# First k-tile's shift and scale by matmuls on TensorE in a hybrid retention layer, with a new order of loads, norms and copies in the front

## The chip, the cores and the metric

The kernel runs on one core of one Trainium2 chip. The metric is device time in microseconds (us) of one launch, the median of several runs. The engines are TensorE (PE; its weight loads are shown as PEld), VectorE (DVE), ScalarE (ACT), GpSimd (POOL) and SyncE (SP), which issues most of the DMAs. TensorE's clock has two levels, 1.2 and 2.4 GHz; the profile's column PEclk shows the granted clock as a share of the full one.

## What is computed

One layer over 512 latent tokens of width 1024, with 256 context tokens and two conditioning vectors of length 1024. The part that the change touches is the start:

```python
mod   = jax.nn.silu(c)     @ w_ada + b_ada      # 6 * 1024 columns
mod_c = jax.nn.silu(c_ctx) @ w_ada + b_ada
sh1, sc1, g1, sh2, sc2, g2 = jnp.split(mod[:, None, :], N_MOD, axis=-1)
sh1c, sc1c, ... = jnp.split(mod_c, N_MOD, axis=-1)

uc = _modulate(ctx, sh1c, sc1c)                 # _layer_norm(.) * (1 + scale) + shift
...
u = _modulate(x, sh1, sc1)
mix = _token_mixer(u @ w_in, ...)               # retention, pooling, gates, projections
x = _post_norm(ALPHA * x + g1 * mix, ...)
...                                             # modulation, gated MLP with a convolution, post norm
```

## The kernel before

Features lie on the partitions in all large products: `x` (512 x 1024) is loaded in four blocks of 128 rows, normalised, and transposed on TensorE into `xnT`, eight k-tiles of 128 features by 512 tokens. The modulated `u` is split into a high and a low part (`uh`, `ul`), as each weight tile is (`hi`, `lo`), and each product is made in three passes: `wh*uh`, `wl*uh`, `wh*ul`. The conditioning columns lie in `mod` (128 x 48): column j holds features 128j to 128j+127 of silu(c) @ w_ada + b_ada. `mod` column kt is the shift of k-tile kt, column 8+kt its scale. `modc` holds the same for the context, 16 columns.

The front of the program, from the first load to the end of the k-tile loop, stands inside `ordered(*ORDS)`: on each of the five engines the instructions keep the order in which the program writes them. So a line that is moved in the source is moved on its engine's queue, and whatever stands behind a waiting instruction waits too. The order in the source of before is this:

- `load_x`, `load` of c, ident and bada, and `first_load(0)` (L242 to L254) put the loads on SP's queue.
- For each row block, `x_stats` (L280) takes statistics on VectorE (L132, L123); GpSimd makes the reciprocal root (L125, L126) and the product L283. `x_norm` (L286) is one instruction: on ScalarE (L290) it waits for L283, on VectorE (L292) for L126. `x_trans(tb, g)` (L294) transposes one half of a block, four 128 x 128 transposes into one PSUM bank (L298), and a copy on ScalarE puts them into `xnT` (L318 to L350).
- `silu_row` (L108) broadcasts silu(c) over the partitions by eight transposes into two banks (L117), and ScalarE copies them into an SBUF row (L118). The dot products of the front read the banks; later ones read the row.
- `warm(n)` (L301) issues n filler matmuls in bf16 on zeros (L304).
- `first_matvec(j)` (L255) makes one column of `mod`: two products with sum of 128 x 512 on VectorE (L258), and L260 adds the parts and the bias.
- The first k-tile is prepared in L329 to L349: `uh` on ScalarE (L339), the weights' casts (L341) and low parts, `u` (L344) and the subtraction for `ul` (L83) on VectorE. `held` are transposes whose copies come later (L350, L367).
- The loop over the eight k-tiles (L359) has TensorE's 18 matmuls of a k-tile in `g0_mm` (L352, L356), 6 feature tiles by 3 passes, and prepares the next k-tile by `first_prep` (L267): the weights' split (cast on ScalarE L88, low part on GpSimd L83), two calls of `first_matvec`, and `modulate` (L225, L228). At k-tile 6 `ctx_mod(0)` (L387) makes the context's columns 0 and 8 on VectorE.

Behind the loop come the other projections, `mm3` (L92 to L95), the retention, and the MLP. `L641` and `L644` are small fp32 matmuls of the retention: the loop at L643 issues four of L644 per head.

## Time and profile before

| | us |
|---|---|
| median of 3 runs | 829.94 |
| lowest, highest | 828.57, 830.37 |
| the profiled execution's own time | 828.57 |
| its span in the profile | 826.8 |
| TensorE busy | 801.3 |
| VectorE busy | 537.5 |
| GpSimd busy | 401.6 |
| ScalarE busy | 365.1 |

The profile shows one execution, the fastest of the three. Its span runs from the first to the last instruction; the run's own time has 1.77 us more around it. A busy TensorE is not one at its peak, since its ends are modelled. In the rows further down, "idle before <-releaser" is the time for which the engine had nothing to do before that instruction, and what ended it.

### The profile page before, as it was taken

The numbers are of one execution on the slowest core, as the hardware profiler recorded it, in microseconds if no ns is written. First come the engines' busy times: TensorE is split into PE (matmuls) and PEld (weight loads), VectorE is DVE, ScalarE is ACT, GpSimd is POOL, SyncE is SP. The second block draws the span as 40 slices with busy tenths as digits, with TensorE's granted clock in tenths as the row PEclk, the third lists the DMA queues.
The fourth block names the chain that finished last, engine by engine and source line by source line (L and its number), as shares of the span: only waits on it lengthen the run. The fifth ranks groups of instructions, "written<-read, shape, count | busy, mean of one in ns | idle before, by whom it ended". The sixth has DMA issues, their size and how long they took to land.

```text
span 826.8 us, 10600 instructions
## 1 busy us (share of the span) xinstructions
PE 801.3 (97%) x3865; PEld 668.9 (81%) x3865; DVE 537.5 (65%) x1040; ACT 365.1 (44%) x579; POOL 401.6 (49%) x295
## 2 busy tenths in 40 slices
PE   6989999999999999999999999999999999999995
PEld 4768877888888888888788998888888888888884
DVE  7947789884267773333667579887778877522147
ACT  4644526221454343323325476665566556233101
POOL 3754360021443242104624779988888888321106
PEclk9999999999999999999999999999999999999998
DMA  9950359973220006460504512322232222343002
GB/s 342 405 199 1 140 205 328 324 259 120 75 77 26 1 2 253 133 201 9 205 21 185 192 38 85 117 83 97 103 103 102 83 97 102 102 153 102 1 1 101
DMA packets 34356, 106.94 MB, mean 129 GB/s; under 512 B 4592, under 2 KB 5376, under 8 KB 34304
## 3 DMA queue, kind: packets, MB, share of 16 engines
q1 hardware_dynamic: 34304, 106.27, 36.7%
q8 instruction: 30, 0.49, 0.2%
q14 instruction: 22, 0.18, 0.1%
HBM read 104.14 MB, written 2.11 MB: 129 GB/s over the span
## 4 chain that ended last, share of the span: by engine, by line
PE 87%; DVE 5%; POOL 2%; ACT 2%; issue 2%; DMA 1%; POOLq 0%; SPq 0%; DVEq 0%; ACTq 0%
PE ps L95 26%; PE ps L94 26%; PE ps L93 26%; PE ps L356 3%; PE ps L674 1%; PE ps L644 1%; PE ps L675 1%; POOL S L83 1%; DVE raw L205 1%; DVE S L258 1%; DVE lo L83 1%; PE ps L636 1%; DMA S<-in_x 1%; PE ps L641 1%; POOL lo L83 1%
## 5 line engine op out<-in xcount | busy, mean ns | idle before, releaser
L95 PE MATMUL ps<-S,lo 128*128 128x512 f32 (+1 forms) x560 | 216.4, 388 | 4.2 <-POOL lo L83 3.2
L93 PE MATMUL ps<-S,hi 128*128 128x512 f32 (+1 forms) x560 | 218.2, 390 | 1.0 <-ACT hi L88 1.0
L94 PE MATMUL ps<-S,hi 128*128 128x512 f32 (+1 forms) x560 | 217.1, 388 | 0.0
L83 POOL TENSOR_TENSOR lo<-raw,hi 128x1024 fp32r<-128x1024 f32 (+3 forms) x61 | 141.2, 2317 | 154.6 <-ACT hi L88 152.0
L998 DVE SCALAR_TENSOR_TENSOR t<-ps,convw,t 128x441 f32<-128x441 f32 (+1 forms) x258 | 163.8, 690 | 45.3 <-POOL t L996 45.1
L88 ACT CAST hi<-raw 128x1024 fp32r<-128x1024 f32 (+1 forms) x96 | 99.3, 1035 | 176.1 <-PE ps L95 61.3
L95 PEld LDWEIGHTS ps<-S,lo 128*128 128x128 f32 x560 | 105.6, 189 | 26.9 <-POOL lo L83 4.0
L93 PEld LDWEIGHTS ps<-S,hi 128*128 128x128 f32 x560 | 105.5, 188 | 22.6 <-ACT hi L88 1.5
L94 PEld LDWEIGHTS ps<-S,hi 128*128 128x128 f32 x560 | 105.6, 189 | 21.2
L996 POOL TENSOR_TENSOR t<-t,t 128x448 f32<-128x448 f32 x88 | 101.9, 1158 | 34.4 <-ACT t L1081 31.0
L95 PE MATMUL ps<-S,S 128*128 128x512 f32 (+1 forms) x308 | 112.2, 364 | 0.0
L94 PE MATMUL ps<-S,S 128*128 128x512 f32 (+1 forms) x308 | 112.2, 364 | 0.0
L93 PE MATMUL ps<-S,S 128*128 128x512 f32 (+1 forms) x308 | 111.4, 365 | 0.0
L83 DVE TENSOR_TENSOR lo<-raw,hi 128x1024 fp32r<-128x1024 f32 x37 | 47.2, 1276 | 68.0 <-ACT hi L88 68.0
L94 PE MATMUL ps<-lo,S 128*128 128x512 f32 x208 | 81.0, 390 | 0.0
L95 PE MATMUL ps<-hi,S 128*128 128x512 f32 x208 | 80.8, 389 | 0.0
L93 PE MATMUL ps<-hi,S 128*128 128x512 f32 x208 | 77.2, 391 | 1.6 <-ACT S L546 1.0
L83 POOL TENSOR_TENSOR S<-raw,S 128x1024 fp32r<-128x1024 f32 x21 | 50.6, 2410 | 38.9 <-ACT S L765 23.5
L1078 ACT ACTIVATE t<-ps,convb,convw 128x512 f32<-128x512 f32 x43 | 33.6, 781 | 75.2 <-PE ps L95 75.2
L93 PEld LDWEIGHTS ps<-S,S 128*128 128x128 f32 x308 | 58.1, 189 | 9.2
L94 PEld LDWEIGHTS ps<-S,S 128*128 128x128 f32 x308 | 58.1, 189 | 9.2
L95 PEld LDWEIGHTS ps<-S,S 128*128 128x128 f32 x308 | 58.1, 189 | 9.1
(219 smaller groups left out, 1065.3 us busy)
## 6 DMA issues: line engine op xcount, KB each, us to landing
raw<-in_w_up SPq DMA_DIRECT2D x44, 512.0 KB, 3.3
raw<-in_wada SPq DMA_DIRECT2D x32, 512.0 KB, 5.3
raw<-in_w_down SPq DMA_DIRECT2D x22, 512.0 KB, 3.3
S<-in_wada SPq DMA_DIRECT2D x16, 512.0 KB, 9.6
raw<-in_w_v SPq DMA_DIRECT2D x16, 256.0 KB, 4.5
raw<-in_w_ga SPq DMA_DIRECT2D x8, 512.0 KB, 4.3
raw<-in_w_gb SPq DMA_DIRECT2D x8, 512.0 KB, 3.3
raw<-in_w_br SPq DMA_DIRECT2D x8, 512.0 KB, 4.0
```

The costliest lines, as they stand in the source:

```text
L83: eng.tensor_tensor(out, x, y, ALU.subtract)
L88: act.copy(hi, raw)
L93: pe.matmul(out, lhsT=sh, rhs=mh, start=first, stop=False)
L94: pe.matmul(out, lhsT=sh, rhs=ml, start=False, stop=False)
L95: pe.matmul(out, lhsT=sl, rhs=mh, start=False, stop=last)
L205: dve.scalar_tensor_tensor(out_junk, raw, 1.0, silu_c, ALU.mult, ALU.mult, accum_out=mod[:, j:j + 1])
L258: dve.scalar_tensor_tensor(junk[:, cs], ada_slot(j)[:, cs], 1.0, silu_h[hf], ALU.mult, ALU.mult, accum_out=dst[:, j:j + 1])
L356: pe.matmul(g0[f], lhsT=w[:, f * P:(f + 1) * P], rhs=m[:, kt, :], start=kt == 0 and i == 0, stop=kt == NKT - 1 and i == 2)
L636: pe.matmul(score[h + i][:, ns], lhsT=kT[half_rows, t, ns], rhs=qT[half_rows, t, ns], start=True, stop=True)
L996: pool.tensor_tensor(o, o, i, ALU.add)
L998: dve.scalar_tensor_tensor(o, i, w, o, ALU.mult, ALU.add)
L1078: act.activation(acc, src, AF.Identity, bias=convb[:, i:i + 1], scale=convw[:, i, 4:5])
```

## The change

- `w_ada`'s tiles 0 and 8 come to the device transposed (`wada_t`), and `c` and `c_ctx` as two columns for each k. `pe_matvec(i)` makes shift (i = 0) and scale (i = 1) of the first k-tile by eight matmuls of 128 x 2 each on TensorE, which add up in a bank `mv`, for c and c_ctx at once. `put_matvec` adds the bias on VectorE. The two calls of `first_matvec` for k-tile 0 go, and with them `ctx_mod(0)` at k-tile 6.
- c, ident and bada are loaded from ScalarE's queue; SP begins with the four blocks of x.
- Block 0's norm goes from VectorE to ScalarE, in halves; the first half of block 2's from ScalarE to VectorE. `x_trans(0, 1)` stands earlier. The last group of fillers, `warm(N_W)`, goes.
- `first_u` makes `uh` and `u` of the first k-tile in pieces of 384 and 128 columns; the second reads the bank of block 3's transposes.
- ScalarE's two copies of silu's banks into the SBUF row stand behind the copies of the held transposes in the loop's first turn.

```diff
--- before.py
+++ after.py
@@ -105,9 +105,8 @@
     dve.memset(neg_half, -0.5)
     keep("gap0", [P, 24])
 
-    def silu_row(cols):
-
-        t = row()
+    def silu_banks(cols):
+
         halves = []
         for hf in range(2):
             ps = bank()
@@ -115,8 +114,7 @@
             for j in range(4):
                 k = 4 * hf + j
                 pe.transpose(ps[:, j * P:(j + 1) * P], cols[:, k:k + 1].broadcast_to([P, P]), ident)
-            act.copy(t[:, hf * SEQ:(hf + 1) * SEQ], ps)
-        return t, halves
+        return halves
 
     def ln_scale(st):
         mv = small([P, 2])
@@ -234,22 +232,22 @@
         for j in (kt, 8 + kt):
             matvec2(modc, part[:, 1], j, ada_slot(j), silu_ch)
 
-    cols = cbuf[:, 3072:3072 + 3 * NKT].rearrange("p (i k) -> p i k", i=3)
+    cols = cbuf[:, 3072:3072 + 5 * NKT].rearrange("p (i k) -> p i k", i=5)
 
     def load_x(tb):
         load(xs[:, tb, :], a["x"][tb * P:(tb + 1) * P, :])
 
-    load_x(0)
-    load(cols[:, 0], a["c"])
-    ident = load(keep("ident", [P, P]), a["ident"])
-    for tb in range(1, NTB):
+    ident = keep("ident", [P, P])
+    bada = keep("bada", [P, 48])
+    act.dma_start(cols[:, 0:2], a["c"])
+    act.dma_start(ident, a["ident"])
+    act.dma_start(bada, a["bada"])
+    for tb in range(NTB):
         load_x(tb)
 
-    bada = load(keep("bada", [P, 48]), a["bada"])
-
     def first_load(kt):
-        for j in (kt, 8 + kt):
-            load(ada_slot(j), a["wada"][j])
+        for i, j in enumerate((kt, 8 + kt)):
+            load(ada_slot(j), a["wada"][j] if kt else a["wada_t"][i])
         return load(raw4((P, NF0)), a["w_first"][kt])
 
     def first_matvec(j):
@@ -279,7 +277,7 @@
 
     def x_stats(tb):
         mu, rs = ln_stats(xs[:, tb, :])
-        nmr = cols[:, 2, tb:tb + 1]
+        nmr = cols[:, 4, tb:tb + 1]
         pool.tensor_scalar(nmr, mu, rs, -1.0, ALU.mult, ALU.mult)
         stats[tb] = mu, rs, nmr
 
@@ -306,48 +304,74 @@
     idle = t2(dt=mybir.dt.bfloat16)
     pool.memset(idle, 0.0)
     lo_half, hi_half = slice(0, SEQ), slice(SEQ, D)
+    def pe_matvec(i):
+
+        wt = ada_slot(8 * i).rearrange("p (k f) -> p k f", k=NKT)
+        for k in range(NKT):
+            pe.matmul(mv[:, 2 * i:2 * i + 2], lhsT=wt[:, k, :], rhs=cols[:, 2:4, k],
+                      start=k == 0, stop=k == NKT - 1)
+
+    def put_matvec(m, n):
+        for i in range(2):
+            j = 8 * i
+            dve.tensor_scalar(m[:, j:j + 1], mv[:, 2 * i + n:2 * i + n + 1], bada[:, j:j + 1], None, ALU.add)
+
     x_stats(0)
-    act.activation(cols[:, 1], cols[:, 0], AF.Sigmoid)
-    dve.tensor_tensor(cols[:, 1], cols[:, 0], cols[:, 1], ALU.mult)
-    silu_c, silu_h = silu_row(cols[:, 1])
+    act.activation(cols[:, 2:4], cols[:, 0:2], AF.Sigmoid)
+    dve.tensor_tensor(cols[:, 2:4], cols[:, 0:2], cols[:, 2:4], ALU.mult)
+    silu_h = silu_banks(cols[:, 2])
     x_stats(1)
-    x_norm(0, dve)
+    for cs in (lo_half, hi_half):
+        x_norm(0, act, cs)
     front = [x_trans(0, 0)]
     warm(2)
+    held = [x_trans(0, 1)]
+    x_stats(2)
     x_norm(1, act, lo_half)
     act.copy(*front[0])
     x_norm(1, act, hi_half)
     front.append(x_trans(1, 0))
     warm(2)
-    x_stats(2)
-    x_norm(2, act, lo_half)
-    act.copy(*front[1])
-    front.append(x_trans(2, 0))
-    x_stats(3)
-    held = [x_trans(0, 1)]
     for j in (8, 32):
         dve.tensor_scalar(bada[:, j:j + 8], bada[:, j:j + 8], 1.0, None, ALU.add)
-    first_matvec(0)
+    x_stats(3)
+    act.copy(*front[1])
+    mv = bank()
+    x_norm(2, dve, lo_half)
+    pe_matvec(0)
+    front.append(x_trans(2, 0))
+    act.copy(*front[2])
+    held.append(x_trans(1, 1))
+    pe_matvec(1)
     x_norm(3, dve, lo_half)
-    act.copy(*front[2])
+    put_matvec(mod, 0)
     front.append(x_trans(3, 0))
+    wh, wl = (sb.tile([P, NF0], F32R, tag=t, bufs=2, name=nm(t)) for t in ("hi", "lo"))
+    first, last = slice(0, 3 * P), slice(3 * P, SEQ)
+
+    def first_u(out, eng):
+
+        for cs, src in ((first, xnT[:, 0, first]), (last, front[3][1][:, 0, :])):
+            if eng is act:
+                act.activation(out[:, cs], src, AF.Identity, bias=mod[:, 0:1], scale=mod[:, 8:9])
+            else:
+                dve.tensor_scalar(out[:, cs], src, mod[:, 8:9], mod[:, 0:1], ALU.mult, ALU.add)
+
+    dve.tensor_copy(wh[:, lo_half], raw0[:, lo_half])
+    put_matvec(modc, 1)
+    first_u(uh[:, 0, :], act)
     act.copy(*front[3])
-    held.append(x_trans(1, 1))
-    warm(N_W)
-    first_matvec(8)
-    wh, wl = (sb.tile([P, NF0], F32R, tag=t, bufs=2, name=nm(t)) for t in ("hi", "lo"))
-    act.activation(uh[:, 0, :], xnT[:, 0, :], AF.Identity, bias=mod[:, 0:1], scale=mod[:, 8:9])
-    for cs, cp in ((lo_half, dve.tensor_copy), (slice(SEQ, NF0), act.copy)):
-        cp(wh[:, cs], raw0[:, cs])
+    act.copy(wh[:, SEQ:NF0], raw0[:, SEQ:NF0])
+    for cs in (lo_half, slice(SEQ, NF0)):
         sub(pool, wl[:, cs], raw0[:, cs], wh[:, cs].bitcast(F32))
     u = t2()
-    dve.tensor_scalar(u, xnT[:, 0, :], mod[:, 8:9], mod[:, 0:1], ALU.mult, ALU.add)
+    first_u(u, dve)
     sub(dve, ul[:, 0, :], u, uh[:, 0, :].bitcast(F32))
     for tb in (2, 3):
         x_norm(tb, dve, hi_half)
-    ready = wh, wl
     for h in held:
         act.copy(*h)
+    ready = wh, wl
 
     def g0_mm(kt, fs, passes=range(3)):
         for i in passes:
@@ -365,6 +389,9 @@
             g0_mm(kt, range(0, 4), range(2, 3))
             for h in held:
                 act.copy(*h)
+            silu_c = row()
+            for hf, cs in enumerate((lo_half, hi_half)):
+                act.copy(silu_c[:, cs], silu_h[hf])
             g0 += [bank() for _ in range(N_G0)]
             ready = first_prep(1, first_load(1))
         elif kt + 1 < NKT:
@@ -384,7 +411,6 @@
             silu_ch = [bank() for _ in range(2)]
             for hf in range(2):
                 dve.tensor_tensor(silu_ch[hf], silu_cc[:, hf * SEQ:(hf + 1) * SEQ], gate_c[hf], ALU.mult)
-            ctx_mod(0)
 
     qk = slot(0, [P, 2, 4, SEQ])
     qT, kT = qk[:, 0], qk[:, 1]
@@ -1246,9 +1272,10 @@
     a = {}
     a["x"] = i["x"][0]
     a["ctx"] = i["ctx"][0]
-    a["c"] = i["c"].reshape(NKT, P).T
+    a["c"] = np.stack([i[n].reshape(NKT, P).T for n in ("c", "c_ctx")], 1)
     a["c_ctx"] = i["c_ctx"].reshape(1, D)
     a["wada"] = i["w_ada"][0].T.reshape(48, P, D)
+    a["wada_t"] = i["w_ada"][0].reshape(NKT, P, 48, P)[:, :, (0, 8)].transpose(2, 1, 0, 3).reshape(2, P, D)
     a["bada"] = i["b_ada"][0].reshape(48, P).T
     lgt = i["ret_decay_logit"][0]
     a["logit"] = np.concatenate([np.broadcast_to(lgt.reshape(1, 16), (P, 16)),
```

What this makes of the order is shown at three places. The first is TensorE's queue in the front. Of before, from the first transposes of x (bank ps_134 is block 0's first half, ps_145 block 1's, ps_164 block 2's, ps_178 block 0's second half, t_11 the fillers' operand):

```order
L298 MATMUL ps_134<-ident,S_6_76 128x128 [waits DVE_49]
L298 MATMUL ps_134<-ident,S_6_76 128x128 x3
L304 MATMUL ps_139<-t_11_98 128x512
L304 MATMUL ps_139<-t_11_98 128x512
L298 MATMUL ps_145<-ident,S_6_76 128x128 [waits DMAHW3_49,Activation_49]
L298 MATMUL ps_145<-ident,S_6_76 128x128 x3
L304 MATMUL ps_150<-t_11_98 128x512
L304 MATMUL ps_150<-t_11_98 128x512
L298 MATMUL ps_164<-ident,S_6_76 128x128 [waits DMAHW4_49,Activation_49]
L298 MATMUL ps_164<-ident,S_6_76 128x128 x3
L298 MATMUL ps_178<-ident,S_6_76 128x128 x4
L298 MATMUL ps_190<-ident,S_6_76 128x128 [waits DMAHW5_49,DVE_49,PE_49]
```

Of the change (ps_132 and ps_140 are block 0's halves, ps_157 block 1's first, ps_187 block 2's first, ps_193 block 1's second; S_2_72 holds the transposed weights, S_1_71 silu's columns):

```order
L296 MATMUL ps_132<-ident,S_6_76 128x128 [waits DMAHW1_49,Activation_49]
L302 MATMUL ps_137<-t_11_98 128x512
L302 MATMUL ps_137<-t_11_98 128x512
L296 MATMUL ps_140<-ident,S_6_76 128x128 [waits Activation_49]
L296 MATMUL ps_157<-ident,S_6_76 128x128 [waits DMAHW3_49,Activation_49]
L302 MATMUL ps_162<-t_11_98 128x512
L302 MATMUL ps_162<-t_11_98 128x512
L311 MATMUL ps_177<-S_1_71,S_2_72 128x2 [waits DMAHW7_49]
L311 MATMUL ps_177<-S_1_71,S_2_72 128x2 x7
L296 MATMUL ps_187<-ident,S_6_76 128x128 [waits DMAHW5_49,DVE_49,PE_49]
L296 MATMUL ps_193<-ident,S_6_76 128x128 [waits Activation_49]
L311 MATMUL ps_177<-S_1_71,S_2_72 128x2 [waits DMAHW0_49]
```

The second half of block 0 moved up ahead of block 1, and the two groups of eight matmuls stand between the transposes of blocks 0 to 2 and that of block 3.

The second place is ScalarE around the end of the first k-tile's preparation. Of before (ps_178 and ps_196 are held transposes of blocks 0 and 1, ps_235 and ps_240 of blocks 2 and 3):

```order
L339 ACTIVATE S_8_78<-S_7_77,mod 128x512 [waits DVE_49,Activation_49]
L341 CAST hi_209<-raw_91 128x256 [waits DMAHW1_49]
L350 COPY S_7_77<-ps_178 128x4x128
L350 COPY S_7_77<-ps_196 128x4x128 [waits PE_49]
L367 COPY S_7_77<-ps_235 128x4x128 [waits PE_49]
L367 COPY S_7_77<-ps_240 128x4x128 [waits PE_49]
L88 CAST hi_257<-raw_255 128x768 [waits DMAHW6_49]
L225 ACTIVATE S_8_78<-S_7_77,mod 128x512 [waits DVE_49]
```

Of the change (ps_111 and ps_116 are the two banks of silu, row_261 the SBUF row):

```order
L356 ACTIVATE S_8_78<-S_7_77,mod 128x384 [waits DVE_49,Activation_49]
L356 ACTIVATE S_8_78<-ps_209,mod 128x128 [waits PE_49]
L363 COPY S_7_77<-ps_209 128x4x128
L364 CAST hi_214<-raw_91 128x256 [waits DMAHW1_49]
L373 COPY S_7_77<-ps_140 128x4x128
L373 COPY S_7_77<-ps_193 128x4x128
L391 COPY S_7_77<-ps_245 128x4x128 [waits PE_49]
L391 COPY S_7_77<-ps_250 128x4x128 [waits PE_49]
L394 COPY row_261<-ps_111 128x512
L394 COPY row_261<-ps_116 128x512
L88 CAST hi_270<-raw_268 128x768 [waits DMAHW6_49]
L223 ACTIVATE S_8_78<-S_7_77,mod 128x512 [waits DVE_49,Activation_49]
```

The two copies of silu's banks stand behind the copies that wait for TensorE, and ahead of the cast and the modulation of the second k-tile; before, they were ScalarE's second and third instruction.

The third place is VectorE from the first k-tile's columns to the second k-tile's dot products. Of before (ps_112 is silu's first bank, hi_209 the weights' high part):

```order
L260 TENSOR_SCALAR mod<-mod,part,bada 128x1 [waits DVE_49]
L341 CAST hi_209<-raw_91 128x512 [waits DMAHW1_49]
L344 TENSOR_SCALAR t_38_216<-S_7_77,mod 128x512 [waits DVE_49,Activation_49]
L83 TENSOR_TENSOR S_9_79<-t_38_216,S_8_78 128x512 [waits DVE_49,Activation_49]
L292 TENSOR_SCALAR S_6_76<-S_6_76,sm_156,sm_158 128x512
L292 TENSOR_SCALAR S_6_76<-S_6_76,sm_172,sm_174 128x512
L258 SCALAR_TENSOR_TENSOR S_1_71,mod<-S_2_72,ps_112 128x512 [waits DMAHW4_49]
L258 SCALAR_TENSOR_TENSOR S_1_71,part<-S_2_72,ps_118 128x512
```

Of the change (ps_177 is `mv`, ps_209 block 3's transposes, ps_111 and ps_116 silu's banks):

```order
L317 TENSOR_SCALAR mod<-ps_177,bada 128x1 [waits PE_49]
L317 TENSOR_SCALAR mod<-ps_177,bada 128x1
L360 CAST hi_214<-raw_91 128x512 [waits DMAHW1_49]
L317 TENSOR_SCALAR modc<-ps_177,bada 128x1 x2
L358 TENSOR_SCALAR t_37_225<-S_7_77,mod 128x384 [waits DVE_49,Activation_49]
L358 TENSOR_SCALAR t_37_225<-ps_209,mod 128x128 [waits PE_49,Activation_49]
L83 TENSOR_TENSOR S_9_79<-t_37_225,S_8_78 128x512 [waits DVE_49]
L290 TENSOR_SCALAR S_6_76<-S_6_76,sm_148,sm_150 128x512
L290 TENSOR_SCALAR S_6_76<-S_6_76,sm_170,sm_172 128x512
L256 SCALAR_TENSOR_TENSOR S_1_71,mod<-S_2_72,ps_111 128x512 [waits DMAHW4_49,Activation_49]
L256 SCALAR_TENSOR_TENSOR S_1_71,part<-S_2_72,ps_116 128x512 [waits Activation_49]
```

The dot products' first two instructions now wait for ScalarE, where before they waited for their load alone, and `u`'s second piece waits for TensorE and ScalarE.

## Rows read from the trace of the kernel before

**Rows 1.** The page: busy time and share of an engine, the chain by engine.

```profile
PE 801.3 (97%) x3865; PEld 668.9 (81%) x3865; DVE 537.5 (65%) x1040; ACT 365.1 (44%) x579; POOL 401.6 (49%) x295
...
PE 87%; DVE 5%; POOL 2%; ACT 2%; issue 2%; DMA 1%; POOLq 0%; SPq 0%; DVEq 0%; ACTq 0%
```

**Rows 2.** Stretches in us: busy time of each engine, PEclk, DMA share, GB/s.

```profile
24.00:52.00 28.00, 28.00 (x124) 22.78 (x122) 24.57 (x77) 16.09 (x24) 19.83 (x13) 1.00 0.92 360
...
56.00:60.00 4.00, 4.00 (x12) 3.15 (x12) 0.06 (x1) 0.00 (x0) 2.08 (x1) 0.60 0.63 187
```

**Rows 3.** The chain that ended last, 3 to 24 us: start, us, what.

```profile
15.11 0.28 DVE mod L260
...
15.48 0.82 ACT S L339
...
16.33 1.54 DVE S L83
...
19.20 1.22 DVE S L258 x4
```

**Rows 4.** Timeline of PE, 5 to 24 us: start, us, line, [idle before <-releaser].

```profile
5.66 1.97 PE L117 MATMUL ps<-ident,S 128*128 128x128 f32 x8 [5.66 <-DVE S L311]
9.02 1.11 PE L298 MATMUL ps<-ident,S 128*128 128x128 f32 x4 [1.39 <-DVE S L292]
9.92 1.06 PE L304 MATMUL ps<-t 128*128 128x512 bf16 x2
...
14.87 1.03 PE L304 MATMUL ps<-t 128*128 128x512 bf16 x4
...
18.89 1.08 PE L298 MATMUL ps<-ident,S 128*128 128x128 f32 x8 [0.33 <-DVE S L292]
19.74 1.64 PE L356 MATMUL ps<-S,hi 128*128 128x512 f32 x6
...
21.67 0.61 PE L356 MATMUL ps<-S,hi 128*128 128x512 f32 x2
23.15 1.21 PE L356 MATMUL ps<-S,hi 128*128 128x512 f32 x4 [0.86 <-ACT S L225]
```

**Rows 5.** Timeline of ACT, 3 to 23 us.

```profile
6.81 0.59 ACT L118 COPY row<-ps 128x512 f32<-128x512 f32 x1 [2.41 <-PE ps L117]
...
10.10 0.81 ACT L290 ACTIVATE S<-S,S,sm 128x512 f32<-128x512 f32 x1 [1.85 <-POOL S L283]
...
16.50 1.06 ACT L350 COPY S<-ps 128x512 f32<-128x512 f32 x2
19.56 1.07 ACT L367 COPY S<-ps 128x512 f32<-128x512 f32 x2 [2.00 <-PE ps L298]
```

**Rows 6.** Timeline of POOL, 3 to 14 us.

```profile
6.63 0.27 POOL L283 TENSOR_SCALAR S<-sm,sm 128x1 f32<-128x1 f32 x1
```

**Rows 7.** SP's loads of line 98, 4.7 to 5.5 us: issues, and time to landing.

```profile
L98 SPq DMA_DIRECT2D S<-in_wada x2: 551/815/1079, 4.0 to 5.1; - x2
...
DMA to landing us min/median/max: 6.8/6.9/7.0
```

**Rows 8.** Timeline of PE, 48 to 62 us.

```profile
53.35 0.50 PE L93 MATMUL ps<-S,hi 128*128 128x512 f32 x1 [1.04 <-ACT hi L88]
...
55.79 0.50 PE L95 MATMUL ps<-S,lo 128*128 128x512 f32 x1 [1.71 <-POOL lo L83]
...
56.82 0.61 PE L93 MATMUL ps<-S,hi 128*128 128x512 f32 x1
...
60.22 0.42 PE L95 MATMUL ps<-S,lo 128*128 128x512 f32 x1
```

**Rows 9.** The chain that ended last, 222 to 227 us.

```profile
225.77 0.89 PE ps L644 x8
```

**Rows 10.** Timeline of DVE, 3 to 24 us.

```profile
8.20 0.76 DVE L292 TENSOR_SCALAR S<-S,sm,sm 128x1024 f32<-128x1024 f32 x1
...
11.71 0.19 DVE L329 TENSOR_SCALAR bada<-bada 128x8 f32<-128x8 f32 x2
```

## Prediction

> **What bounds the kernel now.** The first look goes to the page's busy times and its chain of waits: TensorE is busy for 97% of the span and makes up 87% of the chain [rows 1]. So an edit on another engine counts only where TensorE waits for it, and the next view is the stretches: from 24 to 52 us TensorE is busy for 28.00 of 28.00 us [rows 2]. Whatever moves the start of that stretch therefore moves the end of the program by as much, unless the idle times of 1.04 and 1.71 us before 53.35 and 55.79 take some of it back [rows 8]. Those are waits for ScalarE's and GpSimd's splits of later weights, which follow the same loop; I take them to move rigidly.
>
> The stretch starts with the second k-tile, at 23.15 us [rows 4]. The chain of waits before it [rows 3] runs on VectorE: the second column of the first k-tile is finished by L260 at 15.11, ScalarE modulates at 15.48, VectorE subtracts at 16.33, normalises twice, starts the second k-tile's dot products at 19.20, and ScalarE's L225 lets TensorE go at 23.15 [rows 4]. TensorE itself ends the first k-tile at 21.67 + 0.61 = 22.28 and stands for 0.86 us [rows 4]. The change is priced by what it does to 15.11, to the 4.0 us from there to the dot products, and to the wait in front of these.
>
> **(a) The first shift and scale come later: +1.2 us.** Removed on VectorE are the two columns' dot products (1.22 + 0.28 = 1.5 us each) [rows 3] and the 0.76 us norm of row block 0; the norm, at 8.20, and the products stood on the chain [rows 3, 10]. In their place stands a chain on TensorE. ScalarE's norm of the first half can start when GpSimd's L283 ends, 6.63 + 0.27 = 6.90 [rows 6], takes 0.81 at L290 [rows 5], and TensorE transposes from about 7.8. Four transposes take 0.90 there (9.92 - 9.02) [rows 4], two fillers at the lower clock 2 x 0.43 (eight 512-column matmuls fill 3.40 us from 56.82 to 60.22) [rows 8]. So: 7.8, fillers 8.7, the hoisted second half 9.5, block 1's first half 10.4, the second pair of fillers 11.3. Before, TensorE ran slow until its second pair of fillers: a pair at 9.92 takes 1.06 us, four at 14.87 take 1.03 [rows 4]. I let the clock rise with the second pair again, which ends near 11.7. The weights are not late: `w_ada`'s two tiles were issued at 4.0 and 5.1 and landed 6.8 to 7.0 us later, by 12.1 [rows 7], and now stand behind three fewer small loads on SP.
>
> The trace has no fp32 matmul of two columns. The nearest row is L644, eight records in 0.89 us, 0.111 each [rows 9]: narrow fp32 matmuls whose weight load sets the pitch. The loop at L643 issues four matmuls for these eight records, so an fp32 matmul that is no transpose makes two, and eight matmuls are 16 x 0.111 = 1.78 us. Then 11.7 + 1.8 = 13.5, eight transposes 0.85 (19.74 - 18.89) [rows 4] to 14.4, the second eight to 16.2, and L317 reads them at about 16.3 against 15.11: +1.2. Lower bound: records that cost nothing, since two columns are little beside 512 in 0.226 us (28.00 / 124) [rows 2]; that takes 3.6 off and gives -2.4. Upper bound: all records at the 0.225 us of a slow transpose, +5.7 in place of +1.2, where the fillers, four instead of eight, no longer raise the clock. I take the middle, the row nearest in shape.
>
> **(b) VectorE's stretch to the dot products: +0.9.** New on it are two small sums for the context's columns (0.19 for two of that kind, L329) [rows 10] and `u` in two pieces. The second piece reads the bank of front[3] behind ScalarE's copy of it. ScalarE starts 0.37 after the column is there (15.48 - 15.11) [rows 3], needs some 0.85 for its two pieces and 0.53 for the copy (1.06 for two) [rows 5], so the piece ends near 17.2 on the old time scale, where the subtraction began at 16.33 [rows 3]: +0.9. The norms behind it are the same two. At the least it is +0.2 (the small sums alone), if the wait is short.
>
> **(c) A new wait in front of the dot products: +2.0.** The copies of the silu row stood on ScalarE at 6.81, long done [rows 5]. Now they stand behind the two copies of the held transposes, and the order shows what hangs on them: VectorE's first product of the second k-tile waits for ScalarE, since both read the same bank. Before, it waited for its load alone. The two copies ran from 19.56 for 1.07 [rows 5]; they follow transposes that follow VectorE's norms, so they shift with (a) and (b). The silu copy ends 0.53 after 20.63, at 21.15 on the old scale, and the product stood at about 19.2 [rows 3]: +2.0. The second product waits for the second copy, to 21.7, which the first covers. Queued behind the waiting product are both columns of the second k-tile, hence ScalarE's modulation and TensorE's second k-tile: all of it passes to the end. Bounds: nothing if VectorE came 2 us later anyway, 2.6 if the second copy binds too.
>
> The same copies push ScalarE's L88 split back by 1.1 us, to 22.6 on the old scale; GpSimd's low parts come then at 24.5, and TensorE's first pass, which wants only the high parts, runs to about 26 there. That is hidden.
>
> **(d) TensorE's clock: +1.6.** TensorE's stand before the second k-tile grows from 0.86 to about 2.9 us (21.67 + 0.61 + 2.1 = 24.4, start near 27.25). Such a stand is in the trace: after idle times of 1.04 and 1.71 us close together the granted clock of 56 to 60 us is 0.60 [rows 2, 8], and eight matmuls take 3.40 us, 0.425 each, where 124 take 28.00, 0.226 each [rows 2]. That costs 8 x 0.2 = 1.6 us. I take it once; the lower bound is nothing, the upper twice that.
>
> **Parts at nothing.** VectorE's removed products and the norm it loses: TensorE's chain and the wait (c) take their place. The dropped context columns of k-tile 0 at the sixth k-tile, some 3 us of VectorE: TensorE is busy without a gap there [rows 2]. The small loads on ScalarE's queue: three issues in front of its first activation, whose result VectorE needs for TensorE's first start at 5.66 [rows 4]. If they are late, the silu transposes start late, and meet idle TensorE before 9.02 (5.66 + 1.97 = 7.63, so 1.4 us). The half norm of block 2 that VectorE takes over is half of 0.76 us [rows 10], in a stretch that now waits for TensorE. Behind the second k-tile the order of every engine is that of before.
>
> **Sum.** 1.2 + 0.9 + 2.0 + 1.6 = +5.7 us. The profiled execution took 828.57 (span 826.8) and would take 834.3; the median of the runs, 829.94, lies 1.37 above it, so I forecast 835.6. A difference under 0.2%, 1.66 us, is about what a measurement of this kernel cannot tell from none.
>
> **Rivals.**
> 1. *The clock does not fall.* The stand of (d) is one piece, the known one two. Then +4.1, 834.0. For it: idle stretches before 9.02 and around 16 us cost the clock nothing visible. Against: it is longer than either piece that did.
> 2. *The clock stays low through both products.* Twelve transposes from 5.66 to 9.92 ran at about 0.22 to 0.25 us each and did not raise it; it rose only among fillers [rows 4], of which four are left, between transposes. Then (a) is +5.7 and the sum +10.2: 840. The Trainium skill, "TensorE: Matmul & The Clock Gate", section "Part 4: PE-mode transpose", says a transpose does not count as TensorE work for the clock in the same way; the row at 5.66 agrees, and by the page alone I would put this rival first.
> 3. *Not slower: the matvecs' records run far below a weight load.* With the clock held, as in rival 1, the sum is 4.1 less 32 records by what each falls short of 0.111 us. It comes within 1.66 us at 0.035 us for a record and below; at nothing it is +0.5. The middle, +1.1, gives 831.0. For it: the row of 0.111 multiplies 128 columns, this one two. Against: those records, too, have 128 columns of weights to load, and the row is the shortest pitch that I found for fp32 with 128 rows [rows 9]. The Trainium skill, same page, section "Wait — 56ns, not 53.3ns?", gives about 25 ns as the least distance between starts of small matmuls; by that, an estimate, the sum would be +1.3. No row here shows such a pitch.
> 4. *The edit gains.* The wait (c) does not bind, because the second halves of blocks 0 and 1 are transposed ahead and ScalarE comes to its copies early, and the records cost nothing: (a) and (b) at their lower ends, -2.4 + 0.2, give -2.2: 827.7.
>
> **Chances.** Forecast 0.58 (its own range 834 to 838), rival 1 0.18, rival 2 0.08, rival 3 0.10, rival 4 0.06. Slower by over 0.2%: 0.84, the forecast and the first two; within: 0.10, the third; faster: 0.06, the fourth. The range runs from 831.0, rival 3, to 838.5, the forecast with a second fall of the clock (+1.6) and the second copy binding (+0.6) and a little more; it leaves out rivals 2 and 4 and the far ends of the rest, some 2 in 10.
>
> **What will show it.** In the profile after: L317 near 16.3 (a); VectorE's subtraction near 18.4 (b); the first L256 with an idle time of about 2 us in front, released by ScalarE's L394 (c); TensorE standing for about 3 us before its second k-tile at 27.2, and a granted clock near 0.6 behind it (d); L311's records at 0.111 us. It would be wrong with records of 0.03 us, with an L256 without a wait, a second k-tile before 25 us, or a pause at 52 to 56 us that shrinks.

## The result, and the profile after

The changed kernel takes 834.37 us (median of 4 runs, 833.85 to 837.08) beside 830.15 for the kernel before on the same chip: a ratio of 1.0061, interval 1.0036 to 1.0086, slower by some 5 us. (The two medians lie 4.2 us apart; the means, 834.92 and 829.85, lie 5.1 apart, as the ratio has it.) Run again among the experiments it gave 1.0072 (1.0056 to 1.0087).

The first profile is that of its slowest run, 837.08 us, span 835.3, 8.5 longer than the profile before, which is that of the fastest run; so 8.5 is more than the loss. The timeline of TensorE in the front (start, us, engine, line, operation, [idle before <-releaser]):

```profile
6.10 1.94 PE L116 MATMUL ps<-ident,S 128*128 128x128 f32 x8 [6.10 <-DMA ident<-in_ident]
...
12.29 1.84 PE L311 MATMUL ps<-S,S 128*128 128x2 f32 x16
14.00 1.07 PE L296 MATMUL ps<-ident,S 128*128 128x128 f32 x8
14.90 2.73 PE L311 MATMUL ps<-S,S 128*128 128x2 f32 x16
17.49 1.09 PE L296 MATMUL ps<-ident,S 128*128 128x128 f32 x4
...
28.98 1.80 PE L380 MATMUL ps<-S,hi 128*128 128x512 f32 x4 [2.97 <-ACT S L223]
```

The silu transposes wait for ident's load until 6.10 [rows 4 had 5.66, behind VectorE]. L311's first sixteen records take 14.00 - 12.29 = 1.71 us, 0.107 each; the second sixteen take 17.49 - 14.90 = 2.59. The second k-tile starts at 28.98 instead of 23.15 [rows 4], after 2.97 us of idle time. VectorE between the columns and that start:

```profile
17.67 0.34 DVE L317 TENSOR_SCALAR mod<-ps,bada 128x1 f32<-128x1 f32 x2 [5.48 <-PE ps L311]
...
18.52 1.39 DVE L358 TENSOR_SCALAR t<-S,mod 128x384 f32<-128x384 f32 x1
...
20.27 1.03 DVE L83 TENSOR_TENSOR S<-t,S 128x512 fp32r<-128x512 f32 x1
21.22 0.99 DVE L290 TENSOR_SCALAR S<-S,sm,sm 128x512 f32<-128x512 f32 x2
24.88 0.69 DVE L256 SCALAR_TENSOR_TENSOR S<-S,ps 128x512 f32<-128x512 f32 x1 [2.67 <-ACT row L394]
```

VectorE is done with its norms at 22.21 and stands for 2.67 us until ScalarE's L394, the first of the copies of silu's banks, is through. This is the wait of term (c). The chain of work that ended last shows what it hangs on (start, us, engine, what; L391 are the held transposes' copies):

```profile
17.67 0.35 DVE mod L317 x2
...
18.11 1.06 ACT S L356 x2
...
19.21 3.60 PE ps L380 x8
22.82 0.45 PE ps L296 x4
...
23.29 1.08 ACT S L391 x2
24.36 0.49 ACT row L394
...
24.88 1.31 DVE S L256 x4
```

From the columns on, this chain does not pass VectorE's `u` and its norms. The held transposes follow TensorE's first eight passes of the first k-tile, which take 3.60 us at the low clock, and not the norms, which had ended at 22.21. Before, the same eight passes ended at 18.57, after 2.2 us, and the transposes at 18.89 waited for VectorE [rows 4]:

```profile
16.35 1.20 PE L356 MATMUL ps<-S,hi 128*128 128x512 f32 x4 [0.45 <-ACT S L339]
17.39 1.18 PE L356 MATMUL ps<-S,lo 128*128 128x512 f32 x4
```

The stretches (busy time of each engine, PEclk, DMA share, GB/s):

```profile
12.00:16.00 4.00, 4.00 (x36) 3.95 (x34) 0.18 (x1) 0.90 (x2) 0.23 (x1) 0.96 1.03 410
16.00:20.00 4.00, 3.37 (x14) 2.88 (x15) 2.33 (x7) 1.89 (x5) 1.26 (x1) 0.50 1.03 410
...
28.00:32.00 4.00, 3.02 (x8) 2.41 (x9) 3.93 (x14) 3.15 (x5) 2.29 (x2) 0.66 1.03 407
...
148.00:152.00 4.00, 4.00 (x12) 3.22 (x12) 4.00 (x11) 4.00 (x11) 0.00 (x0) 0.60 0.91 294
```

The clock is down in three places where it was up in the kernel before: from inside L311's second group on, behind the start of the second k-tile, and at 148 us, far behind all edits. Lined up matmul by matmul from the end, the profile after lies 5.83 us behind the one before at the second k-tile, 7.12 at 53.35 (its 60.47), 7.07 at 141 and 8.69 at 146: 1.29 us for the second fall of the clock, 1.6 for the third. The third is put down to chance: the same kernel run again has none there, and of the ten profiles below five have it. Just ahead of that place TensorE pauses three times, for 0.64 to 0.72, 0.50 and 0.50 us, in every profile, with the fall and without it.

### The profile page after: what moved, and what is told of

Read it like the earlier page. It is cut to its first block, busy times and chain, and to the rows that moved or that the text cites. A ratio compares the mean times of both kernels' runs of the same rounds, so it can differ in the third digit from the quotient of the medians.

```text
span 835.3 us, 10647 instructions
## 1 busy us (share of the span) xinstructions
PE 808.9 (97%) x3893; PEld 677.9 (81%) x3893; DVE 532.3 (64%) x1025; ACT 365.9 (44%) x581; POOL 400.2 (48%) x295
## 4 chain that ended last, share of the span: by engine, by line
PE 88%; DVE 4%; ACT 2%; POOL 2%; issue 2%; DMA 1%; POOLq 0%; ACTq 0%; DVEq 0%
PE ps L95 26%; PE ps L94 26%; PE ps L93 26%; PE ps L380 4%; PE ps L670 1%; PE ps L700 1%; PE ps L701 1%; POOL S L83 1%; DVE raw L203 1%; DVE S L209 1%; DVE lo L83 1%; DMA ident<-in_ident 1%; PE ps L662 1%; PE ps L667 1%; PE ps L311 1%
## 5 line engine op out<-in xcount | busy, mean ns | idle before, releaser
L83 POOL TENSOR_TENSOR lo<-raw,hi 128x1024 fp32r<-128x1024 f32 (+3 forms) x61 | 140.5, 2303 | 163.2 <-ACT hi L88 156.6
L83 DVE TENSOR_TENSOR lo<-raw,hi 128x1024 fp32r<-128x1024 f32 x37 | 47.4, 1281 | 67.8 <-ACT hi L88 67.7
L83 POOL TENSOR_TENSOR S<-raw,S 128x1024 fp32r<-128x1024 f32 x21 | 50.6, 2414 | 38.8 <-ACT S L791 23.3
```

What stands on the lines that cost most here:

```text
L83: eng.tensor_tensor(out, x, y, ALU.subtract)
```

## The experiments

All ratios are to the kernel before, run beside each on the same chip, the experiments in five rounds. They did not all run on the same chip, so a difference of two ratios carries the intervals of both.

| kernel | ratio (interval) | second k-tile starts, us |
|---|---|---|
| changed, first result | 1.0061 (1.0036 to 1.0086) | 28.98 |
| changed, again | 1.0072 (1.0056 to 1.0087) | 27.66 |
| changed, silu copies early | 1.0016 (1.0007 to 1.0024) | 24.23 |
| before, silu copies late | 1.0046 (1.0034 to 1.0059) | 25.91 |
| changed, columns on VectorE | 1.0049 (1.0037 to 1.0062) | 26.20 |
| changed, four fillers ahead of the second product | 1.0085 (1.0071 to 1.0099) | 26.71 |
| silu copies early, ident first | 1.0018 (1.0005 to 1.0030) | 24.54 |
| silu copies early, columns on VectorE | 0.9998 (0.9989 to 1.0008) | 23.23 |
| silu copies early, u before the cast | 1.0010 (1.0001 to 1.0018) | 23.82 |
| split version | 0.9982 (0.9973 to 0.9991) | 21.87 |
| split version, c first, u before the cast | 0.9975 (0.9966 to 0.9984) | 21.19 |

### The silu copies put back early

```diff
     act.copy(*front[2])
+    silu_c = row()
+    for hf, cs in enumerate((lo_half, hi_half)):
+        act.copy(silu_c[:, cs], silu_h[hf])
     held.append(x_trans(1, 1))
...
-            silu_c = row()
-            for hf, cs in enumerate((lo_half, hi_half)):
-                act.copy(silu_c[:, cs], silu_h[hf])
```

> The changed kernel with the two copies of silu's banks put back ahead of the first modulation on ScalarE (after the copy of block 2's transposes, where ScalarE idles from 15.3 to 18.1 us). Theory: in the changed kernel VectorE waits 2.67 us for them before the second k-tile's products, and TensorE's stand of 2.97 us behind that lets its clock fall. Without the wait VectorE's first product starts at about 22.2 instead of 24.9, TensorE stands for under 0.5 us, and the clock fall behind it (1.3 us) goes: 3 to 4 us less, 830.4 to 831.4. Rival: the late columns and the slow first k-tile hold the second k-tile up anyway; then under 1 us is gained: 833.4 to 834.4.

The ratio falls from 1.0061 (or 1.0072) to 1.0016, by 0.0045 to 0.0056 or 3.7 to 4.6 us. On VectorE and TensorE:

```profile
15.69 0.34 DVE L317 TENSOR_SCALAR mod<-ps,bada 128x1 f32<-128x1 f32 x2 [3.43 <-PE ps L311]
...
16.54 1.41 DVE L361 TENSOR_SCALAR t<-S,mod 128x384 f32<-128x384 f32 x1
...
19.24 0.99 DVE L290 TENSOR_SCALAR S<-S,sm,sm 128x512 f32<-128x512 f32 x2
20.15 0.67 DVE L256 SCALAR_TENSOR_TENSOR S<-S,ps 128x512 f32<-128x512 f32 x1
```

```profile
24.23 1.20 PE L383 MATMUL ps<-S,hi 128*128 128x512 f32 x4 [0.34 <-ACT S L223]
```

The first dot product follows the norms at once, without a wait, and TensorE stands for 0.34 us. Theory: confirmed. The wait and what hangs on it are three quarters of the loss.

### The silu copies late in the kernel before

```diff
-            act.copy(t[:, hf * SEQ:(hf + 1) * SEQ], ps)
...
             for h in held:
                 act.copy(*h)
+            silu_c = row()
+            for hf, cs in enumerate((lo_half, hi_half)):
+                act.copy(silu_c[:, cs], silu_h[hf])
```

> The kernel before with nothing changed but the two copies of silu's banks, which stand behind the copies of the held transposes as in the changed kernel. Theory: VectorE's first product of the second k-tile moves from 19.1 to about 21.2 us, TensorE stands for 2.9 instead of 0.9 us, its clock falls behind that: +2.0 and +1.3 to +1.6, so 833.4 to 833.8 beside 830.15; 832.2 if the clock holds. Rival: the wait is only where the time shows up in the changed kernel, VectorE being late anyway; then no change, 830.2.

1.0046 is +3.8 us, from moving two copies that were off the chain. VectorE's first product and TensorE's second k-tile:

```profile
21.87 0.69 DVE L256 SCALAR_TENSOR_TENSOR S<-S,ps 128x512 f32<-128x512 f32 x1 [1.95 <-ACT row L368]
```

```profile
25.91 1.19 PE L354 MATMUL ps<-S,hi 128*128 128x512 f32 x4 [2.92 <-ACT S L223]
```

```profile
24.00:28.00 4.00, 2.09 (x9) 1.43 (x9) 3.89 (x16) 2.24 (x3) 2.30 (x3) 1.00 1.03 406
28.00:32.00 4.00, 4.00 (x18) 3.29 (x18) 3.93 (x14) 2.85 (x4) 3.43 (x3) 1.00 1.03 409
```

VectorE waits 1.95 us. (0.7 of the 2.76 by which the second k-tile is late come from block 1 of x, whose statistics began at 7.46 instead of 6.75 in this profile.) But the stand of 2.92 us is not followed by a fall of the clock here: PEclk is 1.00 in both stretches. So that part of the expectation did not show in this profile; the fall near 144 us did, at 1.6 us. The wait of 1.95 us explains some 2 of the 3.8 us; what the rest is in the runs that were not profiled is left open.

### The columns on VectorE, late and early copies

The third kernel has `first_matvec(0)` and `first_matvec(8)` for the two `pe_matvec` and the `put_matvec` calls, with the untransposed weights, and `ctx_mod(0)` again, all else as changed. In a second version of it the silu copies stand early as well, behind block 1's second norm on ScalarE.

```diff
-    pe_matvec(0)
...
-    pe_matvec(1)
...
-    put_matvec(mod, 0)
+    first_matvec(0)
+    first_matvec(8)
```

> The changed kernel with the first k-tile's two columns made on VectorE again (four products with sum, untransposed weights, and the context's columns at the sixth k-tile), all else as changed. Theory: VectorE idles from 12.2 to 17.7 us in the changed kernel and has the columns at 15.3; 2.4 us less of delay, and without the narrow matmuls between the transposes TensorE's first k-tile is not slowed more than now (1.6 us less if its clock is up); the wait for the copies and its clock fall stay: 830.4 to 832.0. Rival: the matmuls are not what is late (the row blocks' transposes are): 834.4 within 0.7.

> The changed kernel's other parts alone: columns on VectorE as in the third experiment, and the silu copies early on ScalarE (behind block 1's second norm). What is left of the change is the loads on ScalarE's queue, the norms shared out otherwise, the moved transposes, the split of the first u and the dropped fillers. Theory: these cost next to nothing; the third experiment's second k-tile at 26.2 comes 2.8 earlier, at 23.4, beside 23.15 before: ratio 0.999 to 1.001. Rival: they carry a cost of their own of 1 us or more (dropped fillers, slow clock): ratio over 1.0015.

With the copies late 1.0049, with the copies early 0.9998. The wait shows in the first and is gone in the second:

```profile
14.87 0.27 DVE L258 TENSOR_SCALAR mod<-mod,part,bada 128x1 f32<-128x1 f32 x1
...
22.11 0.69 DVE L256 SCALAR_TENSOR_TENSOR S<-S,ps 128x512 f32<-128x512 f32 x1 [2.76 <-ACT row L391]
```

```profile
14.75 0.27 DVE L258 TENSOR_SCALAR mod<-mod,part,bada 128x1 f32<-128x1 f32 x1
...
19.14 0.67 DVE L256 SCALAR_TENSOR_TENSOR S<-S,ps 128x512 f32<-128x512 f32 x1
```

The other parts of the change (queue, norms, moved transposes, u in pieces, dropped fillers) show no cost together (0.9989 to 1.0008), and the copies cost the third kernel 0.0051, 4.2 us. The matmuls' own price is what is left between this second version and the first experiment: 1.0016 - 0.9998 = 0.0018 or 1.5 us, with intervals that just touch (1.0007 to 1.0024 and 0.9989 to 1.0008). In the profiles L317 starts at 15.69, where the last column's L258 starts at 14.75 here, and the second k-tile at 24.23 beside 23.23, +1.0. The third kernel as a time came out above its expected 830.4 to 832.0: with a median of 832.99 beside 828.66 it gained 1.0 to 1.9 us on the changed kernel (1.0049 beside 1.0061 to 1.0072) and not the 2.4 to 4 that I had reckoned, since the late columns of the first profile, 17.67, belonged by 1.4 us to that run's own low clock: in the second profile of the changed kernel (below) they come at 16.23.

### Fillers between the products

```diff
+    warm(N_W)
     pe_matvec(1)
```

> The changed kernel with the four dropped fillers put ahead of the second product on TensorE. In its profile the clock is up from 12.2 to 15.7 and down to 22.5 us. Theory: narrow matmuls and transposes do not hold the clock, 512-column fillers do; with it up the second product takes 1.8 in place of 2.6 us and the first k-tile's eight matmuls 1.6 us less, at 0.9 us for the fillers: -1.5, so 832.9. Rival: the clock falls in the same place; then +0.9, 835.3.

```profile
14.24 1.84 PE L311 MATMUL ps<-S,S 128*128 128x2 f32 x16
...
26.71 2.07 PE L381 MATMUL ps<-S,hi 128*128 128x512 f32 x4 [2.99 <-ACT S L223]
```

```profile
22.61 0.69 DVE L256 SCALAR_TENSOR_TENSOR S<-S,ps 128x512 f32<-128x512 f32 x1 [1.96 <-ACT row L395]
```

The clock held: sixteen records in 1.70 us and no fall until 26.4 us. But 1.0085 is no gain; the interval overlaps that of the changed kernel's second run, so whether the fillers cost their 0.9 us is left open. What bounds there is VectorE's wait (its L256 stood for 1.96 us), not TensorE's first k-tile. The expected 1.5 us did not come in the time. In this profile the second k-tile starts 0.95 us before that of the changed kernel's second profile (26.71 beside 27.66), and the wait is 0.8 shorter: with the clock up the first eight passes took 2.5 us (17.66 to 20.17).

### The changed kernel again

> The changed kernel itself, unaltered, as a control beside the others: 1.0061 of the kernel before, within 0.2%. Its profile tells whether the fall of the clock during the second product (15.7 us in the first profile) and the one behind TensorE's stand of 3 us (29.3 us) come again. Theory: the one behind the stand does, since three of four profiles with such a stand show it; the earlier one depends on where in the narrow work the clock is looked at and may be absent. Rival: both are a matter of chance and the stand does not matter.

```profile
14.35 1.84 PE L311 MATMUL ps<-S,S 128*128 128x2 f32 x16
16.06 0.63 PE L296 MATMUL ps<-ident,S 128*128 128x128 f32 x4
...
27.66 1.53 PE L380 MATMUL ps<-S,hi 128*128 128x512 f32 x4 [2.98 <-ACT S L223]
```

```profile
16.23 0.34 DVE L317 TENSOR_SCALAR mod<-ps,bada 128x1 f32<-128x1 f32 x2 [4.41 <-PE ps L311]
...
23.56 0.69 DVE L256 SCALAR_TENSOR_TENSOR S<-S,ps 128x512 f32<-128x512 f32 x1 [2.79 <-ACT row L394]
```

```profile
28.00:32.00 4.00, 4.00 (x12) 3.14 (x11) 3.93 (x14) 2.55 (x4) 3.61 (x3) 0.57 1.03 409
```

The second product runs at full clock here, 16.06 - 14.35 = 1.71 us, so the first profile's slow one was that run's own. The first k-tile's first eight passes are slow again, 17.78 to 21.36 us, and the wait of 2.79 us hangs on them as in the first profile. The fall behind the stand of 2.98 us is back: 0.57. Over all profiles: of five with a stand of 2.9 to 3.0 us four show the fall right behind it or at its end, and lined up as above it costs 1.29, 1.29, 1.15 and 1.30 us between the second k-tile and 53 us; the fifth, the kernel before with late copies, loses 0.01. The four are all versions of the changed kernel. Of the six experiments' profiles with a stand of 0.41 us at most, and that of before with 0.86, none shows a fall there.

### Ident first

```diff
-    act.dma_start(cols[:, 0:2], a["c"])
     act.dma_start(ident, a["ident"])
+    act.dma_start(cols[:, 0:2], a["c"])
```

> The changed kernel with the silu copies early (the first experiment's kernel), and on ScalarE's queue ident's load issued ahead of c's. Theory: in the changed kernel TensorE's first transposes wait for ident until 6.1 us (5.7 before), and since transposes, fillers and products follow each other on TensorE, that lands on the columns; with ident about 0.4 us earlier the columns come at 15.3 and the time falls by 0.3 to 0.5 us against the first experiment's ratio of 1.0016, to about 1.0011. Rival: the transposes then wait for c's column or for the norm of block 0 (7.9 us) instead: no change.

```profile
6.76 1.97 PE L116 MATMUL ps<-ident,S 128*128 128x128 f32 x8 [6.76 <-DVE S L321]
```

No gain, 1.0018 beside 1.0016: the transposes now wait for VectorE's silu (L321), at 6.76 instead of 6.03. The rival holds.

### A version of both, and u before the cast

The split version makes the shift by `pe_matvec(0)` and the scale by `first_matvec(8)` at the same time. It also has ident first and the silu copies early, moves the norms of the second halves of blocks 2 and 3 ahead, and puts the four fillers back, ahead of the first k-tile; these lines show the order:

```diff
-    x_norm(2, dve, lo_half)
+    x_norm(2, dve)
     pe_matvec(0)
     front.append(x_trans(2, 0))
+    x_norm(3, dve, lo_half)
+    first_matvec(8)
+    x_norm(3, act, hi_half)
     act.copy(*front[2])
     held.append(x_trans(1, 1))
-    pe_matvec(1)
-    x_norm(3, dve, lo_half)
     put_matvec(mod, 0)
     front.append(x_trans(3, 0))
+    warm(N_W)
...
-    for tb in (2, 3):
-        x_norm(tb, dve, hi_half)
```

> A version of both: ident first, silu copies early, the shift by TensorE's eight matmuls and the scale by VectorE's products at the same time (it idles there from 12.2 us in the changed kernel), block 2's whole norm in VectorE's gap at 10.4, block 3's second half on ScalarE ahead of the columns, four fillers ahead of the first k-tile. Theory: the columns come at 13.6 instead of 15.4 (before), VectorE has no norms left behind the first k-tile, so the second k-tile's products start at about 17 to 18 instead of 19.2 and TensorE's second k-tile at 21 to 22 instead of 23.15: 1 to 2 us under the kernel before, ratio 0.9976 to 0.9988. Rival: TensorE's own first k-tile (transposes, clock) or the loads take over and nothing is gained: ratio 1.000.

```profile
17.79 0.68 DVE L256 SCALAR_TENSOR_TENSOR S<-S,ps 128x512 f32<-128x512 f32 x1
```

```profile
21.87 1.19 PE L383 MATMUL ps<-S,hi 128*128 128x512 f32 x4 [0.41 <-ACT S L223]
```

0.9982, faster than both kernels: VectorE's dot products for the second k-tile start at 17.79 (19.13 before) and TensorE's second k-tile at 21.87. Which of its edits gains how much is not separated.

The next kernel goes back to the first experiment, for VectorE's slow first piece of u; its edit is also in the last version:

```diff
+    u = t2()
+    dve.tensor_scalar(u[:, first], xnT[:, 0, first], mod[:, 8:9], mod[:, 0:1], ALU.mult, ALU.add)
     dve.tensor_copy(wh[:, lo_half], raw0[:, lo_half])
```

> The first experiment's kernel (silu copies early) with the first piece of u ahead of the weights' cast on VectorE; nothing else. In the first experiment that piece (128x384) took 1.41 us, where it took 0.47 in the kernels whose columns VectorE makes; it lies there beside GpSimd's subtraction of the first weights, which the cast lets go. Theory: VectorE's operation is held while GpSimd works, so ahead of the cast it takes 0.47; the second piece then waits for ScalarE's copy, and the subtraction starts 0.2 to 0.4 us earlier after the column: ratio about 1.0012 beside 1.0016. Rival: the piece is slow for its own sake (its two column operands come fresh): it stays at 1.4, no change.

In the first experiment GpSimd's subtraction ran from 16.46 to 17.73, and VectorE's piece from 16.54 to 17.95:

```profile
16.46 1.27 POOL L83 TENSOR_TENSOR lo<-raw,hi 128x512 fp32r<-128x512 f32 x1 [4.15 <-DVE hi L363]
```

```profile
15.76 0.48 DVE L365 TENSOR_SCALAR t<-S,mod 128x384 f32<-128x384 f32 x1
...
17.31 0.41 DVE L372 TENSOR_SCALAR t<-ps,mod 128x128 f32<-128x128 f32 x1 [0.48 <-ACT S L368]
17.75 0.73 DVE L83 TENSOR_TENSOR S<-t,S 128x512 fp32r<-128x512 f32 x1
18.41 1.41 DVE L290 TENSOR_SCALAR S<-S,sm,sm 128x512 f32<-128x512 f32 x2
```

Ahead of the cast the piece takes 0.48 instead of 1.41: the theory holds, it was held by GpSimd. From the column (15.31) to the subtraction (17.75) it is 2.44 us, beside 18.30 - 15.69 = 2.61, so 0.17 us earlier, just under the 0.2 expected. The second piece waits for ScalarE's copy (0.48 us), and the norms behind, beside GpSimd now, take 1.41 instead of 0.99: from the column to the first dot product it is 4.43 us, beside 4.46. The 1.0010 lies within the first experiment's interval, so no gain is shown.

> The split version (shift on TensorE, scale on VectorE, silu copies early) with c's load ahead of ident's again and u's first piece ahead of the weights' cast. Theory: with c first TensorE's first transposes start at 6.0 instead of 6.6 us, as in the changed kernel, but VectorE's products, which set the columns, follow the statistics of x, so little of it passes on; with the earlier u the second k-tile starts 0.2 to 0.8 us before the split version's 21.87: ratio 0.9970 to 0.9982. Rival: TensorE's first k-tile, with 0.41 us of idle time behind it, is the bound: 0.9982 unchanged.

```profile
20.47 1.92 PE L384 MATMUL ps<-S,hi 128*128 128x512 f32 x6
```

0.9975, 2.1 us under the kernel before, and the second k-tile 0.68 us before the split version's, as expected. The row at 20.47 runs from the last pass of the first k-tile into the second without idle time: TensorE is the bound there now, and the second k-tile starts at 21.19. The two ratios' intervals overlap, and the two edits were not run apart.

## Why the prediction was right, point by point

The forecast was +5.7 us and 835.6; measured were +5 to +6 (1.0061 and 1.0072), with 834.37 and 835.49 as medians. Taken apart along the way from the columns to 53 us, the two profiles of the changed kernel lie behind the one before by:

| us | forecast | first profile | second profile |
|---|---|---|---|
| L317 beside L260 at 15.11 (a) | 1.2 | 2.56 | 1.12 |
| from there to the first dot product, 4.02 before (b and c) | 2.9 | 3.19 | 3.31 |
| from there to the second k-tile | 0 | 0.08 | 0.08 |
| fall of the clock behind it (d) | 1.6 | 1.29 | 1.30 |
| in all, at 53 us | 5.7 | 7.12 | 5.81 |

In the kernel before, the stretch of 4.02 us ends with these two:

```profile
17.79 1.42 DVE L292 TENSOR_SCALAR S<-S,sm,sm 128x512 f32<-128x512 f32 x2
19.13 0.68 DVE L258 SCALAR_TENSOR_TENSOR S<-S,ps 128x512 f32<-128x512 f32 x1
```

The lines of a column of the table add up to its last one by the way they are read; what they tell is how each compares with the forecast. All four parts exist, and the wait of (c) is the largest. That the sum of the second profile comes within 0.1 us is in part luck: (b) and (c) together are 0.4 too small, (d) is 0.3 too large, and (b) turned out not to lie on the chain in these two profiles.

- **(a), +1.2.** L317 comes at 16.23 in the second profile, as forecast (16.3), and at 17.67 in the first, where TensorE was slow for longer (the fillers at 11.49 took 0.97 us, 0.60 in the second profile) and the clock fell in the second product. Beside columns on VectorE, with all else as changed, the matmuls cost 1.5 us by the ratios, +1.0 at the second k-tile. The records cost 0.107 us, as the nearest row had it [rows 9], and rival 3, with 0.035 and below, falls with that. Of rival 2, the low clock through the products, half came in one profile (the second product of the first one, 2.59 in place of 1.71 us) and nothing in the second.
- **(b), +0.9.** From the column to the end of the norms it is 22.21 - 17.67 = 4.54 us, 4.02 before: +0.5. The mechanism was another one. I let the second piece of u wait for ScalarE's copy; in the trace the first piece is held for 0.9 us by GpSimd's subtraction (1.39 beside 0.47), and the norms behind it take 0.99 instead of 1.42. With u ahead of the cast it is the other way round. The contention moves along this stretch, and its sum hardly changes. And in both profiles of the changed kernel the stretch is not on the chain: the dot products wait for the copies, and those for TensorE.
- **(c), +2.0.** The wait is 2.67 and 2.79 us in the changed kernel's profiles, 1.95 with the copies alone moved in the kernel before, 1.96 with the four fillers. The step that failed is "they follow transposes that follow VectorE's norms": the transposes in front of the copies follow TensorE's first eight passes, which the low clock made longer (3.6 us instead of 2.2), and I had kept them at their old length. Where the clock was up, in the last two of these four, the transposes waited for the norms and the size came as forecast. The dropped fillers, to which the forecast gave no term here, go with that clock: in all seven profiles without four fillers ahead of the first k-tile or of the second product the clock fell between 15.6 and 18.1 us, and in the five with them there was no fall before 26.4. One edit, in one profile, puts back the fillers alone. With transposes and narrow products alone the clock fell at 15.7 in the first profile and at 16.8 us in the first experiment; with four fillers between it held until 26.4. The Trainium skill, "TensorE: Matmul & The Clock Gate", section "Part 4: PE-mode transpose", by which transposes do not count for the clock as other TensorE work does, agrees with these rows as far as they go. No run tells the transposes' part from that of the narrow products.
- **(d), +1.6.** Four of five profiles with such a stand show the fall behind it, at 1.15 to 1.30 us, one does not (rival 1). The mechanism is right more often than not and the size a little less than taken. That the stand lets the clock fall rests on this count alone and is not shown; no run fills the stand without removing it, and the one profile without the fall is the only one of a version of the kernel before. The two pauses from which the forecast took this term, 1.04 and 1.71 us, stand in the last version's profile too (before 51.52 and 53.96), and the clock does not fall there (PEclk 1.00 from 52 to 60 us).
- **At nothing.** The rest alone is 0.9998. Two things meet in it: its columns come 0.36 us earlier than before (14.75 for 15.11), and from there to the first dot product it takes 4.39 us instead of 4.02. So (b) is no part of the 1.5 us of (a), since both kernels compared there have it (4.46 and 4.39). The later ident (6.10 for 5.66) starts TensorE's silu transposes 0.4 us later, and moving it forward gains nothing because c then comes later.
- **Rival 4**, that the wait does not bind, is refuted by the first two experiments.

## What to carry to other kernels

When a hand-written order is changed, look at what each moved instruction reads, too: two copies off the chain, moved behind a wait on ScalarE, held up a reader of the same PSUM bank on VectorE and cost 3.7 to 4.6 us in the changed kernel and 3.8 in the one before, more than the matmuls they came with. Moving a small product to TensorE saves VectorE's time only if VectorE was the one that came last; here a version with one column on each engine was faster than both kernels, where either alone was not; it has other edits too, and no run shows the gain of the two engines by itself. And the length of a wait is set by the last thing to end on any way that leads to it: here that was TensorE's first passes at the low clock, and not the norms on the engine that then stood waiting. And a copy that must be made is put where its engine idles, before the next wait and not behind it.

## What was not expected

- VectorE's 128x384 operation with two column operands took 1.41 us while a GpSimd subtraction ran, and 0.48 without it. It began 0.08 us after GpSimd's and ended 0.2 us after it. The Trainium skill, "SBUF — State Buffer", section "🔬 SBUF: two separate sides", describes an exclusive lock on a pair of ports that GpSimd shares with certain VectorE operations, by which the later one stands until the first is done; the rows agree with that.
- TensorE's clock falls in some executions and not in others, in places that no edit touched: at 137 to 149 us in five of the experiments' profiles and the first one of the changed kernel, at some 1.6 us each, and the fall at 57 us of the kernel before [rows 8] is missing in two. That is as much as the smaller terms here, so single profiles are to be compared stretch by stretch and not by their spans.
- A profile without that fall can lose as much further on. In the second profile of the changed kernel TensorE waits 0.25 and 0.72 us for low parts of weights (VectorE's L83) at 185.99 and 194.03, where the first profile and that of before have no wait, and it ends 7.2 us behind the one before instead of 5.8. In the profile with u before the cast such a wait is 0.85 us.
